# HGRN2 attention with both directions in one interleaved tile, 1024-wide DeltaNet steps, and modulation sums that end before HGRN2

## The chip, the cores and the metric

The kernel runs on one core of one Trainium2 chip. The metric is the device time of one execution in microseconds (us), the median of several runs. TensorE does the matrix products (PE in the rows, PEld for its weight loads), VectorE (DVE) and ScalarE (ACT) the elementwise work, GpSimd (POOL) a few memsets and part of the transfers, SyncE (SP) issues most of the transfers.

## The reference

One layer of a hybrid block over 256 latent tokens of width 2048, with 256 context tokens ahead of them. A modulation, computed from a conditioning vector by a product with `w_ada`, scales and shifts the tokens; one projection `w_in` feeds three token mixers: Hyena (a long convolution through a Fourier transform), HGRN2 (a gated linear recurrence, forwards and backwards) and a gated DeltaNet (forwards and backwards). Their outputs are projected, gated, merged and normalised; a squared-ReLU MLP of width 8192 follows. Cut to what the change touches:

```python
mod = silu(c) @ w_ada + b_ada                 # six parts; parts 2..5 are needed after the mixers
# HGRN2, per head and direction, by chunks:
att = einsum('tk,sk,tsk->ts', q, k, exp(cumsum(log f)_t - cumsum(log f)_s), s <= t)
o   = (q * exp(cumsum)) @ state + att @ v     # the two directions are summed
# DeltaNet, per chunk of 64: (I + strict_lower(kb k^T * decay)) is inverted by substitution
```

## The kernel before

All products with weights are made in three passes: `wsplit` (L141) loads a block of 128x1024 floats (512 KB) into a `wraw` buffer through SP's queue (L143), ScalarE rounds it (`whi`, L138), VectorE takes the remainder (`wlo`, L139), and TensorE multiplies high by high, high by low and low by high. There are four `wraw` buffers, four `whi` and three `wlo`. `wload` (L162) is called for every such block; before its own load it advances side jobs.

A side job is a Python generator that `beside` puts in with a rate, `go_on` gives a new rate, and `finish` runs to its end on the spot. At rate 0.55 each `wload` emits 0.55 steps of the job ahead of its weight load. Program order is therefore written out by hand. The framework then fixes the order on each engine by a timeline of its own: among the instructions that are ready it takes the one that is earliest in program order, and so lower work can fill an engine that would stand.

The stages, in program order:

- the first modulation, then `dn_early` (L642): DeltaNet's keys, queries, values and gates, with 24 calls of `wload`.
- `hyena(0)` and `hyena(1)` (L835, called at L913 and L915): six projections each (24 calls of `wload`), the Fourier products, and 12 steps of `fill` (L811), each one block of the output gates (L799 to L801). 72 calls in all.
- `hgrn_group(g)` (L921) for four groups of two heads. Each projects values (L932 to L935), both forget gates (`proj_cm_ctx`, L218 to L220) and queries: 16 calls of `wload`, and in the last group eight more from `fill`. Then come eight levels `lv`. At level `lv` the 256 tokens are cut into pairs of blocks of `1 << lv` tokens, scaled keys `Kt` and queries `Qt` are made (L1021 to L1024), multiplied on TensorE in 128x128 pieces (L1030), and copied under a mask into `att` (L1032); the running products are then extended (L1047 to L1050). Left and right halves of the pairs are separate instructions of 256 columns.
- `dn_inverse` (L742) runs beside the HGRN2 groups at rate 1.3. Its first steps, `dn_systems` (L699), build the matrices `M`; then 62 substitution steps (L756 multiply, L757 add) follow, split in two where they would be wider than 512 columns, with `tmp` in the tag `k2` (six buffers, 512 columns each).
- the gates and `dn_late` (L1160), the branches, `w_out`, and the MLP.

The modulation sums are the side job `ada`, `ada_parts(range(6))` (L500, put in at L780). It has 6 parts of 16 steps. A step loads 512 KB of `w_ada` through SP's queue into a `wraw` buffer (L503; the load of the next step is issued ahead of it), and VectorE multiplies and adds it into `acc` (L514 for the first step of a part, L516 for the 15 others). The part's end stores `acc` through POOL's queue (L518). `acc` lives in the tag `k4`, which has one buffer. `ada` runs at rate 1.0 through `dn_early`, 0.55 through Hyena (L912), 0.1 through HGRN2 (L1074), 0.3 afterwards (L1327), and is finished at L1403, ahead of its use in `ada_cols` (L1122).

Of the kernel before, what the change touches and what calls it, by code (L numbers as in the profile page):

```python
# [11 lines left out]
U8 = mybir.dt.uint8  # L12
# [4 lines left out]
P = 128  # L17
D = 2048
KT = D // P
T = 256  # L20
# [60 lines left out]
def tile_block(ctx: ExitStack, tc: tile.TileContext, A: dict, out: bass.AP):  # L81
# [325 lines left out]
    masks = cst.tile([P, 7, P], U8, name="masks")  # L407
    masks_f = page("masks_f", (7, P))
    dma(out=masks_f, in_=A["masks"])
    nc.vector.tensor_copy(out=masks, in_=masks_f)  # L410
# [331 lines left out]
    def dn_inverse():  # L742

        yield from dn_systems()
        M = dn["M"]
        bI = dn["inst"][:, 1, :]
        for s_ in range(1, 63):
            n = 63 - s_
            parts = 1 if n * s_ <= 512 else 2
            m = -(-n // parts)  # L750
            for a in range(s_ + 1, 64, m):
                b = min(a + m, 64)
                shp = [P, b - a, s_]
                tmp = slot([P, 512], "k2", "tmp")
                tv = tmp[:, 0:(b - a) * s_].rearrange("p (a b) -> p a b", a=b - a)
                tt_(out=tv, in0=bc(M[:, a:b, s_:s_ + 1], shp), in1=bc(M[:, s_:s_ + 1, 0:s_], shp), op=MUL)  # L756
                tt_(out=M[:, a:b, 0:s_], in0=M[:, a:b, 0:s_], in1=tv, op=ADD)  # L757
# [154 lines left out]
    go_on("ada", 0.55)  # L912
# [8 lines left out]
    def hgrn_group(g):  # L921
# [16 lines left out]
        fs, ks = [], []  # L938
        for d, base in enumerate((C_FF, C_FB)):
            pss = proj_cm_ctx(base + g * 256)  # L940
            f, k = page("fk", (2, 512), (2, 512))
            for h in range(2):
                hd = d * 8 + 2 * g + h
                act(out=f[:, h, :], in_=pss[h], func=AF.Sigmoid)
                act(out=k[:, h, :], in_=pss[h], func=AF.Sigmoid, scale=-1.0)
                act(out=f[:, h, :], in_=f[:, h, :], func=AF.Identity, scale=oml[:, hd:hd + 1], bias=lb[:, hd:hd + 1])
                act(out=k[:, h, :], in_=k[:, h, :], func=AF.Copy, scale=oml[:, hd:hd + 1])
            ts_(out=f, in0=f, scalar1=1e-30, scalar2=None, op0=MAX)
            fs.append(f)
            ks.append(k)  # L950
# [5 lines left out]
        for d in range(2):  # L956
            f, k = fs[d], ks[d]
            cp = slot([P, 2, T], "k2", "cp")
            kd, kt_ = k[:, :, T:2 * T], f[:, :, T:2 * T]
            for h in range(2):  # L960
                fc = f[:, h, T:2 * T]
# [23 lines left out]
        PF, SB = fs[0][:, :, 0:T], fs[1][:, :, 0:T]  # L985
        kf, kb_ = ks[0][:, :, 0:T], ks[1][:, :, 0:T]
        SF, PB = ks[0][:, :, T:2 * T], ks[1][:, :, T:2 * T]
        QF, QB = fs[0][:, :, T:2 * T], fs[1][:, :, T:2 * T]
        tt_(out=ksum, in0=kf, in1=kb_, op=ADD)
        ps = sc_ps()  # L990
        for h in range(2):
            for i in range(2):
                sl = slice(i * P, (i + 1) * P)
                mm(ps[:, (2 * h + i) * P:(2 * h + i + 1) * P], ksum[:, h, sl], q[:, h, sl], start=True, stop=True)
        copy(out=att.rearrange("p a b -> p (a b)"), in_=ps)

        def halves(t, b):
            v = t.rearrange("p h (n two b) -> p h n two b", two=2, b=b)
            return v[:, :, :, 0, :], v[:, :, :, 1, :]

        for lv in range(8):
# [3 lines left out]
            n = T // (2 * b)  # L1005
            Kt = slot([P, 2, T], "k2", "Kt")
            Qt = slot([P, 2, T], "k2", "Qt")
            PFl, PFr = halves(PF, b)
            SBl, SBr = halves(SB, b)
            SFl, SFr = halves(SF, b)  # L1010
            PBl, PBr = halves(PB, b)
            kfl, _ = halves(kf, b)
            _, kbr = halves(kb_, b)
            ql, qr = halves(q, b)
            Ktl, Ktr = halves(Kt, b)
            Qtl, Qtr = halves(Qt, b)
            if lv == 0:
                copy(out=Ktl, in_=kfl)
                copy(out=Ktr, in_=kbr)
            else:  # L1020
                tt_(out=Ktl, in0=kfl, in1=SFl, op=MUL)  # L1021
                tt_(out=Ktr, in0=kbr, in1=PBr, op=MUL)
            tt_(out=Qtl, in0=ql, in1=SBl, op=MUL)
            tt_(out=Qtr, in0=qr, in1=PFr, op=MUL)  # L1024
            ps = sc_ps()
            if lv < 7:
                for h in range(2):
                    for i in range(2):
                        sl = slice(i * P, (i + 1) * P)
                        mm(ps[:, (2 * h + i) * P:(2 * h + i + 1) * P], Kt[:, h, sl], Qt[:, h, sl],  # L1030
                           start=True, stop=True)
                nc.vector.copy_predicated(out=att, mask=bc(masks[:, lv:lv + 1, :], [P, 4, P]),  # L1032
                                          data=ps.rearrange("p (a b) -> p a b", a=4))
# [6 lines left out]
            shp = [P, 2, n, b]  # L1040
            if lv == 0:
                copy(out=SFl, in_=PFr)
                nc.gpsimd.memset(SFr, 1.0)
                copy(out=PBr, in_=SBl)
                nc.gpsimd.memset(PBl, 1.0)
            elif lv < 7:
                tt_(out=SFl, in0=SFl, in1=bc(PFr[:, :, :, b - 1:b], shp), op=MUL)  # L1047
                tt_(out=PBr, in0=PBr, in1=bc(SBl[:, :, :, 0:1], shp), op=MUL)
            tt_(out=PFr, in0=PFr, in1=bc(PFl[:, :, :, b - 1:b], shp), op=MUL)
            tt_(out=SBl, in0=SBl, in1=bc(SBr[:, :, :, 0:1], shp), op=MUL)  # L1050
        tt_(out=QF, in0=q, in1=PF, op=MUL)
        tt_(out=QB, in0=q, in1=SB, op=MUL)
# [21 lines left out]
    go_on("ada", 0.1)  # L1074
# [252 lines left out]
    go_on("ada", 0.3)  # L1327
# [215 lines left out]
```

## Time and profile before

| | us |
|---|---|
| three runs, lowest, median, highest | 2389.09, 2390.69, 2390.93 |
| the profiled execution, its own time | 2387.84 |
| its span, first to last instruction | 2385.8 |

| engine | busy us of the span | share | instructions |
|---|---|---|---|
| PE (matmul) | 2285.2 | 96% | 13377 |
| PEld (weight load) | 2003.1 | 84% | 13377 |
| DVE | 1624.5 | 68% | 2119 |
| ACT | 1053.3 | 44% | 1401 |
| POOL | 181.0 | 8% | 297 |

Busy time is the sum of the instructions' spans on an engine. Instructions of one engine overlap at their ends, so what one costs in a dense row of its like is the distance from one start to the next, which is shorter than its own duration. A granted clock (PEclk) of 1.00 is TensorE at 2.4 GHz, 0.5 is 1.2 GHz. One TensorE product of two plain fp32 operands shows as two matmuls in the trace.

### The profile page before, as it was taken

The page shows a single profiled execution, that of the slowest core. Times are in us where ns is not written, and L with a number is a line of the kernel's source. Part 1 is how long each engine was busy: PE and PEld are TensorE (multiplying, and loading weights), DVE is VectorE, ACT ScalarE, POOL GpSimd, SP SyncE. Part 2 cuts the span into 40 slices and gives each one's busy share as a digit, 9 for nine tenths or more (in the row PEclk, how much of TensorE's full clock was granted, in tenths as well). Part 3 has the DMA queues.
Part 4 walks back from the last instruction along what each step waited for, and adds up shares of the span by engine and source line. Part 5 has one row for each costly group of instructions (what it writes and reads, how often), then busy time and mean ns, then how long its engine had stood idle before and what let it go on. Part 6 is the DMA issues. An engine that isn't in the chain of part 4 may idle for free.

```text
span 2385.8 us, 34393 instructions
## 1 busy us (share of the span) xinstructions
PE 2285.2 (96%) x13377; PEld 2003.1 (84%) x13377; DVE 1624.5 (68%) x2119; ACT 1053.3 (44%) x1401; POOL 181.0 (8%) x297
## 2 busy tenths in 40 slices
PE   6999898999999999989999999997999999999998
PEld 4778688989889989777888888886988988988986
DVE  6776467867889898976656656658954555555557
ACT  6665444433433433534443444434444444444442
POOL 0000222000210000012021020000000000000000
PEclk9999999999999999989999999998999999999999
DMA  9958757777663333488786898677876566666664
GB/s 329 344 178 258 229 176 224 242 248 245 196 176 106 116 89 115 124 209 275 227 261 214 284 324 261 202 233 275 303 245 193 181 190 193 181 192 191 191 202 150
DMA packets 296079, 511.30 MB, mean 214 GB/s; under 512 B 17526, under 2 KB 155217, under 8 KB 293324
## 3 DMA queue, kind: packets, MB, share of 16 engines
q1 hardware_dynamic: 271488, 422.63, 56.0%
q0 software_dynamic: 21648, 82.01, 11.1%
q10 hardware_dynamic: 2780, 4.47, 0.5%
q8 instruction: 105, 1.72, 0.3%
q14 instruction: 58, 0.48, 0.1%
HBM read 474.59 MB, written 34.45 MB: 213 GB/s over the span
## 4 chain that ended last, share of the span: by engine, by line
PE 68%; DMA 8%; DVE 5%; ACT 1%; issue 1%; DVEq 0%; SPq 0%; POOL 0%; ACTq 0%
PE mm L220 8%; PE mm L219 8%; PE mm L218 8%; PE mm L475 8%; PE mm L476 8%; PE mm L474 8%; DMA aw<-in_w_ada_dram 3%; PE mm L800 3%; PE mm L801 3%; PE mm L799 3%; DMA wraw<-in_w_in_dram 2%; DVE wlo L139 2%; PE mm L932 1%; PE mm L935 1%; PE mm L934 1%
## 5 line engine op out<-in xcount | busy, mean ns | idle before, releaser
L138 ACT CAST whi<-wraw 128x1024 fp32r<-128x1024 f32 x584 | 613.3, 1052 | 955.0 <-PE mm L219 274.2
L139 DVE TENSOR_TENSOR wlo<-wraw,whi 128x1024 fp32r<-128x1024 f32 x584 | 712.1, 1222 | 452.4 <-PE mm L475 159.6
L220 PE MATMUL mm<-uh,wlo 128*128 128x256 f32 (+1 forms) x1024 | 340.6, 336 | 3.1 <-DVE wlo L139 3.1
L218 PE MATMUL mm<-uh,whi 128*128 128x256 f32 (+1 forms) x960 | 318.3, 332 | 13.8 <-DVE cy L490 13.2
L219 PE MATMUL mm<-ul,whi 128*128 128x256 f32 (+1 forms) x960 | 318.2, 332 | 0.0
L218 PE MATMUL mm<-u,whi 128*128 128x256 f32 x1024 | 290.6, 284 | 5.1 <-ACT u L138 3.8
L219 PE MATMUL mm<-u,whi 128*128 128x256 f32 x1024 | 290.4, 284 | 1.1 <-DVE u L139 1.1
L220 PE MATMUL mm<-u,wlo 128*128 128x256 f32 x1024 | 290.0, 284 | 0.7 <-DVE wlo L139 0.7
L220 PEld LDWEIGHTS mm<-uh,wlo 128*128 128x128 f32 x1024 | 198.3, 194 | 22.4 <-DVE wlo L139 3.8
L218 PEld LDWEIGHTS mm<-uh,whi 128*128 128x128 f32 x960 | 186.5, 194 | 31.1 <-issue 13.9
L218 PEld LDWEIGHTS mm<-u,whi 128*128 128x128 f32 x1024 | 197.4, 193 | 5.8 <-ACT u L138 4.2
L219 PEld LDWEIGHTS mm<-ul,whi 128*128 128x128 f32 x960 | 186.4, 194 | 15.4 <-issue 0.7
L219 PEld LDWEIGHTS mm<-u,whi 128*128 128x128 f32 x1024 | 197.3, 193 | 1.6 <-DVE u L139 1.4
L220 PEld LDWEIGHTS mm<-u,wlo 128*128 128x128 f32 x1024 | 197.0, 193 | 1.1 <-DVE wlo L139 1.1
L476 PE MATMUL mm<-whi,h 128*128 128x512 f32 x480 | 187.2, 390 | 0.0
L475 PE MATMUL mm<-wlo,h 128*128 128x512 f32 x480 | 186.8, 389 | 0.0
L474 PE MATMUL mm<-whi,h 128*128 128x512 f32 x480 | 186.5, 391 | 0.0
L516 DVE SCALAR_TENSOR_TENSOR acc<-aw,csil,acc 128x1024 f32<-128x1024 f32 x90 | 115.2, 1280 | 89.0 <-DMA aw<-in_w_ada_dram 88.7
L800 PE MATMUL mm<-wlo,uh 128*128 128x512 f32 x384 | 152.9, 398 | 4.3 <-DVE wlo L139 4.1
L799 PE MATMUL mm<-whi,uh 128*128 128x512 f32 x384 | 150.1, 400 | 3.3 <-ACT whi L138 1.7
L801 PE MATMUL mm<-whi,ul 128*128 128x512 f32 x384 | 151.2, 394 | 0.0
L474 PEld LDWEIGHTS mm<-whi,h 128*128 128x128 f32 x480 | 90.1, 188 | 19.2 <-issue 0.7
(517 smaller groups left out, 4113.9 us busy)
## 6 DMA issues: line engine op xcount, KB each, us to landing
wraw<-in_w_in_dram SPq DMA_DIRECT2D x264, 512.0 KB, 4.4
wraw<-in_w_ff_dram SPq DMA_DIRECT2D x256, 512.0 KB, 4.0
aw<-in_w_ada_dram SPq DMA_DIRECT2D x96, 512.0 KB, 4.4
raw<-in_w_ada_dram SPq DMA_DIRECT2D x32, 1024.0 KB, 5.6
wraw<-in_w_branch_dram SPq DMA_DIRECT2D x48, 512.0 KB, 5.4
wraw<-in_w_out_dram SPq DMA_DIRECT2D x32, 512.0 KB, 4.8
awr<-in_w_ada_dram SPq DMA_DIRECT2D x32, 512.0 KB, 9.4
g_d<-gate POOLq DMA_DIRECT2D x24, 256.0 KB, 4.6
```

Of the source, the lines that this page charges most:

```text
L138: copy(out=hi, in_=src)
L139: tt_(out=lo, in0=src, in1=hi.bitcast(F32), op=SUB)
L218: mm(ps, wh[:, k, cs], ah, start=first, stop=False, skip_group_check=True)
L219: mm(ps, wh[:, k, cs], al, start=False, stop=False, skip_group_check=True)
L220: mm(ps, wl[:, k, cs], ah, start=False, stop=last, skip_group_check=True)
L474: mm(pss[i], a, wh[:, k, :], start=(kt == 0), stop=False)
L475: mm(pss[i], a, wl[:, k, :], start=False, stop=False)
L476: mm(pss[i], b, wh[:, k, :], start=False, stop=(kt == nk - 1))
L516: stt(out=acc, in0=a, scalar=csil[:, 0, kt:kt + 1], in1=acc, op0=MUL, op1=ADD)
L799: mm(pg[i], a, wh[:, k, :], start=(kt == 0), stop=False)
L800: mm(pg[i], a, wl[:, k, :], start=False, stop=False)
L801: mm(pg[i], c, wh[:, k, :], start=False, stop=(kt == KT - 1))
```

## The change

It has three parts that lie close together in time.

1. HGRN2. The forget gates and keys of both directions go into two tiles `F` and `K` of [2 directions, 2 (latent, context), 2 heads, 256]. `pairs` builds one view that takes the left halves from one direction and the right halves from the other, so that each pair of instructions becomes one of 512 columns. Levels 0 to 5 need only the 64x64 blocks on the diagonal: `blocks` makes eight products with 64 stationary columns and 64 moving ones instead of four of 128 by 128, and the masked copy covers 256 columns instead of 512. Level 6 takes the off-diagonal blocks and writes the full `att` by four copies on ScalarE.
2. DeltaNet. Each substitution step is one multiply and one add, up to 1024 columns wide; `tmp` is taken once and lies in the tag `k4`, with `acc` of the modulation sums.
3. The modulation sums go at 0.61 per `wload` through Hyena instead of 0.55, and `finish("ada")` stands ahead of the first HGRN2 group. The later rates and the `finish` in `modulation2` go away.

```diff
-    masks = cst.tile([P, 7, P], U8, name="masks")
+    masks = cst.tile([P, 6, 64], U8, name="masks")
...
+        tmp = slot([P, 1024], "k4", "tmp")
         for s_ in range(1, 63):
             n = 63 - s_
-            parts = 1 if n * s_ <= 512 else 2
-            m = -(-n // parts)
-            for a in range(s_ + 1, 64, m):
-                b = min(a + m, 64)
-                shp = [P, b - a, s_]
-                tmp = slot([P, 512], "k2", "tmp")
...
+            shp = [P, n, s_]
+            tv = tmp[:, 0:n * s_].rearrange("p (a b) -> p a b", a=n)
+            tt_(out=tv, in0=bc(M[:, s_ + 1:, s_:s_ + 1], shp), in1=bc(M[:, s_:s_ + 1, 0:s_], shp), op=MUL)
+            tt_(out=M[:, s_ + 1:, 0:s_], in0=M[:, s_ + 1:, 0:s_], in1=tv, op=ADD)
             yield
...
-    go_on("ada", 0.55)
+    go_on("ada", 0.61)
     hyena(0)
     fill(0)
     hyena(1)
...
+        F = slot([P, 2, 2, 2, T], "k8", "F")
+        K = slot([P, 2, 2, 2, T], "k8", "K")
...
+        def pairs(t, left, right, b, step=1):
+            v = t[:, 0, 0, 0, 0:1]
+            return bass.AP(tensor=v.tensor, offset=v.offset + left,
+                           ap=[list(v.ap[0]), [2 * b, T // b], [right - left, 2], [step, b]])
+        def blocks(ps, lhs, rhs, other):
+            for h in range(2):
+                for i in range(2):
+                    for f in range(2):
+                        c = i * P + f * 64
+                        r = i * P + (1 - f if other else f) * 64
+                        mm(ps[f * 64:(f + 1) * 64, (2 * h + i) * 64:(2 * h + i + 1) * 64],
+                           lhs[:, h, c:c + 64], rhs[:, h, r:r + 64], start=True, stop=True)
...
-                tt_(out=Ktl, in0=kfl, in1=SFl, op=MUL)
-                tt_(out=Ktr, in0=kbr, in1=PBr, op=MUL)
-            tt_(out=Qtl, in0=ql, in1=SBl, op=MUL)
-            tt_(out=Qtr, in0=qr, in1=PFr, op=MUL)
+                tt_(out=Ktv, in0=pairs(K, KF, KB + b, b), in1=pairs(K, SF, PB + b, b), op=MUL)
+            tt_(out=Qtv, in0=qv, in1=pairs(F, SB, PF + b, b), op=MUL)
             ps = sc_ps()
-            if lv < 7:
...
+            if lv < 6:
+                blocks(ps, Kt, Qt, False)
+                nc.vector.copy_predicated(out=att64, mask=bc(masks[:, lv:lv + 1, :], [P, 4, 64]),
+                                          data=ps[:, 0:T].rearrange("p (a b) -> p a b", a=4))
+            elif lv == 6:
+                blocks(ps, Kt, Qt, True)
+                for f in range(2):
+                    fs, os = slice(f * 64, (f + 1) * 64), slice((1 - f) * 64, (2 - f) * 64)
+                    copy(out=att[fs, :, fs], in_=att64[fs])
+                    copy(out=att[fs, :, os], in_=ps[fs, 0:T].rearrange("p (a b) -> p a b", a=4))
...
     beside("inverse", dn_inverse(), 1.3)
-    go_on("ada", 0.1)
+    finish("ada")
     for g in range(4):
         hgrn_group(g)
...
-    go_on("ada", 0.3)
...
-        finish("ada")
```

## Rows read from the trace of the kernel before

**Rows 1.** Windows: window, its us, busy us (instructions), granted clock, DMA share, GB/s.

```profile
core 0: us, PE busy (x) PEld busy (x) DVE busy (x) ACT busy (x) POOL busy (x), PEclk, DMA share, GB/s
613.00:671.00 58.00, 58.00 (x371) 52.96 (x370) 39.55 (x41) 23.08 (x26) 15.36 (x17) 1.00 0.68 200
740.00:960.00 220.00, 220.00 (x1415) 200.38 (x1414) 199.36 (x371) 86.15 (x129) 1.33 (x4) 1.00 0.34 99
1000.00:1020.00 20.00, 14.72 (x60) 10.99 (x59) 19.32 (x18) 17.84 (x20) 3.08 (x7) 0.91 0.79 185
1040.00:1060.00 20.00, 13.40 (x55) 10.84 (x54) 15.26 (x33) 6.30 (x8) 0.00 (x0) 0.74 0.56 160
1100.00:1120.00 20.00, 17.92 (x88) 12.96 (x87) 13.25 (x18) 5.88 (x8) 4.72 (x10) 1.00 1.03 346
1420.00:1440.00 20.00, 19.61 (x87) 15.92 (x86) 11.30 (x12) 7.37 (x7) 1.61 (x3) 1.00 0.95 351
```

**Rows 2.** Chain that ended last: start us, us, what.

```profile
531.55 1.30 DVE acc L516
...
553.83 1.30 DVE acc L516
...
1027.32 17.71 DMA wraw<-in_w_in_dram
...
1345.83 8.07 DMA aw<-in_w_ada_dram
```

**Rows 3.** Line L516 up to 613 us: durations min/median/max ns, first and last start.

```profile
L516 DVE SCALAR_TENSOR_TENSOR acc<-aw,csil,acc x60: 1150/1283/1287, 153.1 to 611.6; 128x1024 f32<-128x1024 f32 x60
```

**Rows 4.** Page, DMA issues: count, KB each, median us to landing.

```profile
aw<-in_w_ada_dram SPq DMA_DIRECT2D x96, 512.0 KB, 4.4
```

**Rows 5.** Timeline of SP's queue around 613 us: start us, us, line, count.

```profile
609.37 77.11 SPq L143 DMA_DIRECT2D wraw<-in_w_in_dram  x15
687.25 6.06 SPq L503 DMA_DIRECT2D aw<-in_w_ada_dram  x2
```

**Rows 6.** Groups on PE from 613 to 671 us: count, busy us, mean ns.

```profile
L932 PE MATMUL mm<-whi,uh 128*128 128x256 f32 x64 | 18.1, 283 | 0.0
...
L218 PE MATMUL mm<-uh,whi 128*128 128x512 f32 x15 | 5.8, 390 | 0.0
```

**Rows 7.** Timeline of PE at two places: start us, us, line, shape, count.

```profile
733.23 0.28 PE L935 MATMUL mm<-whi,ul 128*128 128x256 f32 x1
733.35 1.06 PE L1030 MATMUL ps<-Qt,Kt 128*128 128x128 f32 x8
734.16 0.36 PE L932 MATMUL mm<-whi,uh 128*128 128x256 f32 x1
734.36 0.28 PE L934 MATMUL mm<-wlo,uh 128*128 128x256 f32 x1
...
1121.57 0.39 PE L800 MATMUL mm<-wlo,uh 128*128 128x512 f32 x1
1121.80 0.39 PE L801 MATMUL mm<-whi,ul 128*128 128x512 f32 x1
1122.12 1.14 PE L1205 MATMUL ps<-XT,VT 64*64 64x64 f32 x16
1123.10 1.09 PE L1200 MATMUL ps<-XN,CT 64*64 64x64 f32 x16
1124.12 0.50 PE L799 MATMUL mm<-whi,uh 128*128 128x512 f32 x1
```

**Rows 8.** Timeline of DVE at two places: start us, us, line, shape.

```profile
626.21 0.68 DVE L876 TENSOR_TENSOR cm<-ps,spl 128x512 f32<-128x512 f32 x1
626.81 0.68 DVE L877 TENSOR_TENSOR cm<-ps,spl 128x512 f32<-128x512 f32 x1
...
1054.83 0.41 DVE L1024 TENSOR_TENSOR Qt<-ivq,fk 128x256 f32<-128x256 f32 x1
1055.16 0.41 DVE L1047 TENSOR_TENSOR fk<-fk 128x256 f32<-128x256 f32 x1
1055.50 0.72 DVE L1032 COPY_PREDICATED hgA<-masks,ps 128x512 f32<-128x512 uint8 x1
```

**Rows 9.** Line L756, the substitution's multiply: durations min/median/max ns, first and last start.

```profile
L756 DVE TENSOR_TENSOR tmp<-M x106: 217/588/686, 687.1 to 996.7; 128x440 f32<-128x440 f32 x6, 128x486 f32<-128x486 f32 x4, 128x480 f32<-128x480 f32 x4, 128x468 f32<-128x468 f32 x4
```

More of the change, by code (lines that the diff above doesn't have):

```diff
@@ L404, in tile_block @@
         step()
-    masks = cst.tile([P, 7, P], U8, name="masks")
+    masks = cst.tile([P, 6, 64], U8, name="masks")
     masks_f = page("masks_f", (7, P))
     dma(out=masks_f, in_=A["masks"])
-    nc.vector.tensor_copy(out=masks, in_=masks_f)
+    for f in range(2):
+        fs = slice(f * 64, (f + 1) * 64)
+        nc.vector.tensor_copy(out=masks[fs], in_=masks_f[fs, 0:6, fs])
     colB = rows_to_cols([
@@ L937, in hgrn_group @@
             copy(out=iv[:, 2 * i:2 * i + 2, :].rearrange("p a b -> p (a b)"), in_=pss[i])
-        fs, ks = [], []
+        F = slot([P, 2, 2, 2, T], "k8", "F")
+        K = slot([P, 2, 2, 2, T], "k8", "K")
         for d, base in enumerate((C_FF, C_FB)):
             pss = proj_cm_ctx(base + g * 256)
-            f, k = page("fk", (2, 512), (2, 512))
             for h in range(2):
                 hd = d * 8 + 2 * g + h
[L944 to L950, printed above, removed]
+                f, k = F[:, 1 - d, :, h, :], K[:, d, :, h, :]
+                pv = pss[h].rearrange("p (s t) -> p s t", s=2)
+                act(out=f, in_=pv, func=AF.Sigmoid)
+                act(out=k, in_=pv, func=AF.Sigmoid, scale=-1.0)
+                act(out=f, in_=f, func=AF.Identity, scale=oml[:, hd:hd + 1], bias=lb[:, hd:hd + 1])
+                act(out=k, in_=k, func=AF.Copy, scale=oml[:, hd:hd + 1])
+            ts_(out=F[:, 1 - d], in0=F[:, 1 - d], scalar1=1e-30, scalar2=None, op0=MAX)
         pq = proj_cm(w_in, C_HQ + g * 256, uxh, uxl)
@@ L982, in hgrn_group @@
             copy(out=S0[:, :, d, :], in_=ps[:, 0:2 * P].rearrange("p (h v) -> p h v", h=2))
[L985 to L989, printed above, removed]
-        ps = sc_ps()
[L991 to L999, printed above, removed]
+        SB, PF, KF, KB, SF, PB = 0, 4 * T, 0, 4 * T, 2 * T, 6 * T
+        def pairs(t, left, right, b, step=1):
[10 more added lines that the diff above has]
+                           lhs[:, h, c:c + 64], rhs[:, h, r:r + 64], start=True, stop=True)
+        tt_(out=ksum, in0=K[:, 0, 0], in1=K[:, 1, 0], op=ADD)
+        ps = sc_ps()
+        blocks(ps, ksum, q, False)
+        att64 = ksum.rearrange("p h t -> p (h t)")[:, 0:T].rearrange("p (a b) -> p a b", a=4)
+        copy(out=att64, in_=ps[:, 0:T].rearrange("p (a b) -> p a b", a=4))
         for lv in range(8):
@@ L1004, in hgrn_group @@
             b = 1 << lv
-            n = T // (2 * b)
             Kt = slot([P, 2, T], "k2", "Kt")
             Qt = slot([P, 2, T], "k2", "Qt")
[L1008 to L1016, printed above, removed]
+            Ktv, Qtv, qv = (t.rearrange("p h (n two b) -> p (h n) two b", two=2, b=b) for t in (Kt, Qt, q))
             if lv == 0:
-                copy(out=Ktl, in_=kfl)
-                copy(out=Ktr, in_=kbr)
-            else:
-                tt_(out=Ktl, in0=kfl, in1=SFl, op=MUL)
-                tt_(out=Ktr, in0=kbr, in1=PBr, op=MUL)
-            tt_(out=Qtl, in0=ql, in1=SBl, op=MUL)
-            tt_(out=Qtr, in0=qr, in1=PFr, op=MUL)
+                copy(out=Ktv, in_=pairs(K, KF, KB + b, b))
+            else:
+                tt_(out=Ktv, in0=pairs(K, KF, KB + b, b), in1=pairs(K, SF, PB + b, b), op=MUL)
+            tt_(out=Qtv, in0=qv, in1=pairs(F, SB, PF + b, b), op=MUL)
             ps = sc_ps()
-            if lv < 7:
[L1027 to L1033, printed above, removed]
+            if lv < 6:
[4 more added lines that the diff above has]
+                blocks(ps, Kt, Qt, True)
+                for f in range(2):
+                    fs, os = slice(f * 64, (f + 1) * 64), slice((1 - f) * 64, (2 - f) * 64)
+                    copy(out=att[fs, :, fs], in_=att64[fs])
+                    copy(out=att[fs, :, os], in_=ps[fs, 0:T].rearrange("p (a b) -> p a b", a=4))
             else:
@@ L1039, in hgrn_group @@
                 copy(out=attx.rearrange("p a c b -> p (a c b)"), in_=ps)
-            shp = [P, 2, n, b]
             if lv == 0:
[L1042 to L1045, printed above, removed]
+                copy(out=pairs(K, SF, PB + b, b), in_=pairs(F, PF + b, SB, b))
+                nc.gpsimd.memset(pairs(K, SF + b, PB, b), 1.0)
             elif lv < 7:
[L1047 to L1052, printed above, removed]
+                t = pairs(K, SF, PB + b, b)
+                tt_(out=t, in0=t, in1=pairs(F, PF + 2 * b - 1, SB, b, 0), op=MUL)
+            t = pairs(F, SB, PF + b, b)
+            tt_(out=t, in0=t, in1=pairs(F, SB + b, PF + b - 1, b, 0), op=MUL)
+        qf = q.rearrange("p h t -> p (h t)").unsqueeze(1)
+        tt_(out=F[:, :, 1].rearrange("p d h t -> p d (h t)"), in0=bc(qf, [P, 2, 2 * T]),
+            in1=F[:, :, 0].rearrange("p d h t -> p d (h t)"), op=MUL)
+        QB, QF = F[:, 0, 1], F[:, 1, 1]
         ps = sc_ps()
```

8 lines of the change are left out of this document (2 added, 6 removed).

## The prediction, made blind

> **What bounds the kernel now.** I read the busy time by stage first, then the chain that ended last, then the queue that feeds the weights, then single instructions. In the heart of HGRN2 TensorE is busy for all of 220 us (740 to 960) at full clock [rows 1], and its matmuls of 512 columns start 0.23 us apart, those of 256 columns 0.12 us apart, with nothing between [rows 7]. VectorE is busy for 199 of the same 220 us, and the DMA engines for a third. So TensorE sets the pace there, and VectorE is close behind. TensorE stands idle at a few places after it: 5.3 us in 1000 to 1020, 6.6 us in 1040 to 1060 (where the granted clock means 0.74) and 2.1 us in 1100 to 1120 [rows 1]. The chain names transfers there: a weight load that took 17.7 us, and later a load of the modulation sums of 8.1 us [rows 2]. Whatever makes VectorE faster can pay only at such places; whatever takes weights away from TensorE costs at once.
>
> **The change, part by part.**
>
> **The modulation sums (part 3)** are the large term. There are 96 loads of 512 KB [rows 4]. By 613 us the trace shows 60 steps of the second to sixteenth kind [rows 3], which are four whole parts with their four first steps: 64 of 96. The program gives the same: 24 calls at 1.0 and 72 at 0.55 are 63.6, and one step is pulled ahead. At 0.61 they are 24 + 43.9, so 67 steps end with Hyena, one more load is under way, and `finish` emits the other 29 steps and 28 loads in one block ahead of every instruction of the first HGRN2 group. In the trace of before, SP's queue sends 15 weight loads between 609 and 687 us before the next two loads of the sums, and the first HGRN2 weights are among these 15 [rows 5]. All weights of the groups now queue behind the 28 loads, in the same four buffers. On VectorE 29 steps of 1.28 us, 37 us, stand ahead of the group's remainders and of `dn_systems`; on POOL's queue two stores of `acc` do. The second part in the block can't start adding until the store of the first has landed, since `acc` has one buffer; the four buffers are then full and the queue waits.
>
> How long the block lasts: 28 loads of 0.524 MB at the best rate in these rows, 351 GB/s at 1420 to 1440 us [rows 1], take 42 us. I add 5 us for the store between the parts (a median load lands in 4.4 us [rows 4]). So the group's first weights leave 47 us later, and TensorE needs another 7 us for landing (4.4 us), rounding and remainder (VectorE's remainder is about as long as a step of the sums); before, the first load left well ahead of its use. What covers these 54 us: in 613 to 671 TensorE was busy for all 58 us, and the group's own matmuls take 3 x 64 x 0.12 = 23 us and 3 x 15 x 0.23 = 10 us of them [rows 6, 7]; L934 and L935 are there as often as L932, L219 and L220 as often as L218. The other 25 us are the tail of Hyena and its gate blocks, whose weights are loaded. TensorE then stands for 54 - 25 = 29 us. Bounds: zero, if group loads get in between; 144 us, if each load waits for the step before it as in 531 to 554 us, where four steps took 22.3 us, 5.6 us each [rows 2]. I take 29, nearer the lower end, since that slow pace belongs to a queue that shared its buffers with weights. After such a stand the clock falls, as in 1040 to 1060 us: the missing quarter of 20 us is 5 us; I add 4 (0 to 5).
>
> Inside Hyena four more steps go in. Each held a buffer for one turn of a queue in which TensorE is nearly fed: +2 us (from 0, if hidden, to 4 x 5.6 = 22, if each costs a whole turn of those in 531 to 554 us).
>
> **The 64x64 blocks (part 1, TensorE).** Before, a level's four products are eight matmuls that start 0.81 us before the next line's, which gives up 0.08 us more: 0.89 us [rows 7]. After, sixteen matmuls of 64x64. The nearest rows have them: sixteen of L1205 and sixteen of L1200 go in 2.00 us; entering costs 0.32 - 0.23 = 0.09 us more than a normal start, leaving is taken to cost the same, so one block is 0.09 + 16 x 0.06 + 0.09 = 1.14 us. That is +0.25 us for each of 8 blocks (one ahead of the levels, levels 0 to 6) in 4 groups: +8 us on an engine that has no slack there. Upper bound: a matmul costs the same with half the columns, 16 x 0.11 + 0.18 = 1.94 us, +34 us in all. Lower bound: the two column halves run side by side, 0.66 us, -7 us in all. I take the measured pace.
>
> The Trainium skill (TensorEngine Tiling (Array Packing), sections Key Properties and Theoretical Speedup) says both things: that a change of tiling mode drains TensorE, and that disjoint halves may run in parallel, up to twice as fast. The trace agrees with the first (0.09 us on entering); the second no row here shows, because the eight products of those rows all lie on one tile. By the second the term would be the lower bound.
>
> **VectorE (parts 1 and 2).** Two instructions of 256 columns take 2 x 0.33 us, start to start, one of 512 takes 0.60 [rows 8], so a merge saves 0.07 us. There are 29 merges a group (2 at level 0, 4 at each of levels 1 to 6, 3 at level 7), 2.0 us. Masked copies shrink: 0.72 us each by their own duration; six at half width save some 2 us, and the seventh goes away. That makes 4.7 us a group, 19 us. The substitution goes from 106 to 62 pairs [rows 9]: 88 instructions x 0.07 = 6 us. The strided views cost nothing more in the rows at hand (0.41 us for both kinds of 1055 us); a view that jumps between two far places at each element is not in the trace, and if it ran at half speed it would eat all of this. Ten steps of the sums that ran between 690 and 1100 us are gone as well: 12 us. So VectorE loses 37 us of work in this stage. Under a TensorE that is busy throughout, none of it is worth anything between 740 and 960 us; there the cover is TensorE's own work, 220 of 220 us.
>
> It counts where TensorE stood. In 1000 to 1060 us the idle 5.3 + 6.6 us and the clock's share (0.09 and 0.26 of 20 us) are 18.9 us. These hang on the end of the inverse, whose last steps and transfers fall into the weights of the last group. An inverse that ends earlier meets projections that ask for half as many weights per us: I take 12 of the 18.9 (0 to 18.9). Later places where the sums' loads stood in the chain (1100 to 1120, 1346): -4 (0 to -6). ScalarE's changes (two copies fewer at level 0, four more at level 6) lie on an engine busy for 39% there: nothing, and if that cover went, sixteen copies at an estimated 0.4 us, VectorE's duration for as many columns, 6 us.
>
> `tmp` in one buffer makes no wait, since multiply and add follow on one engine; but its first use waits for the last store of `acc`. The block of sums ends at about 613 + 47 us, and the substitution began at 687 us: nothing, and what is late next, if it slips, is only the inverse.
>
> **Sum:** 29 + 4 + 2 + 8 - 12 - 4 = +27 us on 2387.84 us, 2414.8. The three runs have their median 2.85 us above the profiled execution: 2417.
>
> **The rivals.** (A) VectorE really bounds HGRN2, and the change pays. For it: 199 of 220 us, and remainders sit between TensorE and its weights. Then the block costs only what VectorE itself stands in it, 47 + 4 - 37 = 14 us, the blocks on TensorE cost nothing, and 37 us of work come off: 14 + 2 - 37 - 4 = -25, 2366 us with the 2.85. It decides if matmuls in 740 to 960 us start later than their own pace allows; the starts 0.12 and 0.23 us apart speak against it.
>
> On this the Trainium skill (Perfetto Trace Analysis, section Identifying the Most-Contended Engine) is sharper than busy time: it calls matmul busy share a poor measure and asks for the weight loads' share, and has the engine of highest occupancy improved first. By it TensorE (200 of 220 us of weight loads) and VectorE (199) stand level, and rival A has its reason; the trace does not decide it beyond the starts.
>
> (B) The block is mostly hidden: the scheduler lets group weights in between, or Hyena's tail is long enough. The gap falls to 6 us without the clock's loss: 6 + 2 + 8 - 16 = 0, 2391 us. For it: the DMA engines are only 68% busy in 613 to 671 us [rows 1]. Against it: program order puts all 28 loads first, and a load of the sums is ready whenever a buffer is free.
>
> (C) The block runs at 5.6 us a step, as in 531 to 554 us. 28 x 5.6 + 5 + 7 - 25 = 144 us of standing: 2387.84 + 144 + 14 - 16 + 2.85, 2533 us.
>
> **How the numbers follow.** No change is within 0.2%, about 4.8 us, which is what a measurement of this kernel can tell: 2385.9 to 2395.5. My forecast has a chance of 0.58, with 2397 to 2442 as its own range (the gap from 12 to 50 us, the blocks and the recovery as bounded); A has 0.24, spread from 2350 to 2385; B 0.12; C 0.06. Faster is A, 0.24; same is B, 0.12; slower is the forecast and C, 0.64. The range leaves out C, half of A and 0.02 of the forecast, 0.20: 2366 to 2444.
>
> **What would show it.** Right: SP's queue sends 28 loads of the sums in a row ahead of the first weights of HGRN2; TensorE stands for some 29 us at about 640 to 675 us with a granted clock below 1.00; sixteen-matmul blocks take 1.1 us; VectorE's share in the groups falls below 0.85 while TensorE stays at 1.00; the stand around 1000 to 1060 us shrinks. The forecast is wrong if group weights come in between the 28 loads, or if the time from the first to the last group shrinks by more than the recovery, which would mean that VectorE set the pace.

## The result, and the profile after

The kernel after takes 2432.94 us (median of 4 runs, 2428.36 to 2436.24), the kernel before 2390.81 in the same comparison: ratio 1.017, 95% interval 1.0145 to 1.0195. The profiled execution has a span of 2432.2 us against 2385.8: 46.4 us more.

Its windows (the columns are those of [rows 1]). The first and the fourth are stretches of [rows 1]; the last is a wider one, since everything from 704 us on lies some 72 us later than before:

```profile
613.00:671.00 58.00, 27.14 (x128) 22.64 (x127) 48.94 (x49) 11.89 (x14) 10.53 (x11) 0.75 0.72 218
671.00:703.00 32.00, 0.00 (x0) 0.00 (x0) 25.55 (x19) 0.00 (x0) 0.00 (x0) 0.50 0.63 212
703.00:740.00 37.00, 35.38 (x235) 33.42 (x236) 30.93 (x42) 10.52 (x11) 2.51 (x5) 0.90 0.63 183
740.00:960.00 220.00, 216.85 (x1485) 191.74 (x1483) 192.35 (x230) 88.49 (x132) 5.26 (x8) 0.99 0.36 100
960.00:1220.00 260.00, 258.80 (x1694) 221.60 (x1693) 160.04 (x191) 132.61 (x181) 30.71 (x45) 1.00 0.63 180
```

The wider window before:

```profile
960.00:1220.00 260.00, 245.71 (x1317) 205.40 (x1316) 186.40 (x272) 116.15 (x158) 40.76 (x64) 0.97 0.74 218
```

Between 613 and 703 us TensorE works for 27 us of 90, and in the last 32 us not at all, at a granted clock of 0.50 (1.2 GHz); before, it was busy for all of 613 to 671. The stands behind the groups are nearly gone: in 960 to 1220 us TensorE stands for 1.2 us at a granted clock of 1.00, against 14.3 us at 0.97 before. So the time is lost in one place and partly won back later. SP's queue around the loss (start us, us to the last issue, line, count), to be set beside [rows 5]:

```profile
605.33 2.26 SPq L143 DMA_DIRECT2D wraw<-in_w_in_dram  x2
609.60 86.52 SPq L505 DMA_DIRECT2D aw<-in_w_ada_dram  x28
697.11 18.06 SPq L143 DMA_DIRECT2D wraw<-in_w_in_dram  x8
```

The 28 loads go out in a row ahead of HGRN2's first weights, as forecast, but in 86.5 us instead of 47. HGRN2's first product, the first line of its values, is a milestone for all that follows (durations min/median/max, first and last start), before and after:

```profile
L932 PE MATMUL mm<-whi,uh x256: 277/283/365, 632.2 to 928.3; 128*128 128x256 f32 x128
```

```profile
L930 PE MATMUL mm<-whi,uh x256: 277/283/580, 704.2 to 1004.6; 128*128 128x256 f32 x128
```

It comes 72.0 us later. From there to the end of the span it is 2385.8 - 632.2 = 1753.6 us before and 2432.2 - 704.2 = 1728.0 after, so 25.6 us are won back: 72.0 - 25.6 = 46.4.

What stretched the loads, in the chain that ended last (start us, us, what):

```profile
660.07 14.99 DMA aw<-in_w_ada_dram
...
676.35 1.27 DVE M L718
...
680.84 1.20 DVE acc L518
682.04 1.12 DVE M L722
...
691.83 1.30 DVE acc L518
...
697.11 5.93 DMA wraw<-in_w_in_dram
```

One load of the sums takes 15 us; then work of `dn_systems` on M (L718, L722, L725) stands between a step at 680.84 and the next at 691.83; the loads wait for the buffers that those steps hold. At its own pace a step takes 1.3 us, as at 691.83. VectorE is busy for most of the block (columns of [rows 1]):

```profile
609.60:696.12 86.52, 30.54 (x140) 25.34 (x138) 72.52 (x68) 12.94 (x15) 10.53 (x11) 0.68 0.68 212
```

Of its 72.5 us some 31 are steps of the sums, some 21 the systems' work on E and M (L712 to L725), and some 20 work of Hyena. The transfers of 645 to 685 us show what shared the DMA engines with the slow load (count, KB each, median us to landing):

```profile
aw<-in_w_ada_dram SPq DMA_DIRECT2D x10, 512.0 KB, 3.5
M<-dk POOLq DMA_DIRECT2D x2, 1024.0 KB, 12.8
acc_d<-acc POOLq DMA_DIRECT2D x1, 512.0 KB, 2.9
br<-bth POOLq DMA_DIRECT2D x2, 256.0 KB, 16.2
```

### The profile page after: what moved, and what is told of

It is laid out like the page before. It is cut to its first block, busy times and chain, and to the rows that moved or that the text cites. A ratio compares the mean times of both kernels' runs of the same rounds, so it can differ in the third digit from the quotient of the medians.

```text
span 2432.2 us, 34716 instructions
## 1 busy us (share of the span) xinstructions
PE 2280.0 (94%) x13633; PEld 1993.9 (82%) x13633; DVE 1609.8 (66%) x1908; ACT 1061.2 (44%) x1409; POOL 180.6 (7%) x293
## 4 chain that ended last, share of the span: by engine, by line
PE 75%; DMA 11%; DVE 8%; issue 5%; ACT 2%; POOL 0%; ACTq 0%; DVEq 0%; SPq 0%; POOLq 0%
PE mm L218 9%; PE mm L219 9%; PE mm L220 9%; PE mm L477 7%; PE mm L478 7%; PE mm L476 7%; DMA aw<-in_w_ada_dram 6%; PE mm L798 3%; PE mm L799 3%; PE mm L797 3%; DMA wraw<-in_w_in_dram 2%; DVE acc L518 2%; DVE wlo L139 2%; PE mm L932 1%; PE mm L930 1%
## 5 line engine op out<-in xcount | busy, mean ns | idle before, releaser
L930 PE MATMUL mm<-whi,uh 128*128 128x256 f32 x256 | 74.3, 291 | 45.5 <-ACT whi L138 45.5
```

## The experiments

The theory after this reading: the third part makes the whole loss, stretched by the systems' work and M's load; the first two parts win. Twelve kernels were run. "First product" is that of HGRN2's values in the profiled run, "the rest" the span from there to the end, which shows the two effects apart. Ratios are to the kernel before on the same chip; its median there was 2385.08 to 2390.81 us, so totals of different rows compare only to within a few us. The two last columns are of one profiled run each.

| run | median us | ratio, 95% interval | first product | the rest |
|---|---|---|---|---|
| before | 2390.81 | 1 | 632.2 | 1753.6 |
| the whole change | 2432.94 | 1.017 (1.0145 to 1.0195) | 704.2 | 1728.0 |
| p3_only | 2441.75 | 1.0223 (1.0194 to 1.0253) | 708.1 | 1731.1 |
| p1_only | 2378.96 | 0.9958 (0.9944 to 0.9971) | 632.9 | 1746.3 |
| p12_page | 2376.08 | 0.9935 (0.9914 to 0.9956) | 625.9 | 1739.5 |
| inv_later | 2433.72 | 1.0189 (1.0156 to 1.0222) | 685.7 | 1745.9 |
| m_held | 2409.27 | 1.0108 (1.0085 to 1.0131) | 676.0 | 1730.1 |
| blocks128 | 2450.59 | 1.028 (1.0257 to 1.0304) | 703.7 | 1744.8 |
| rate100 | 2386.92 | 1.0007 (0.9995 to 1.0019) | 655.3 | 1731.6 |
| rate080 | 2399.37 | 1.0064 (1.004 to 1.0088) | 663.2 | 1734.5 |
| p12_spread | 2382.16 | 0.9975 (0.9962 to 0.9988) | 631.4 | 1746.3 |
| p12_r80 | 2379.94 | 0.9958 (0.9938 to 0.9977) | 641.5 | 1737.9 |
| half_order | 2441.47 | 1.0221 (1.0199 to 1.0243) | 708.3 | 1733.7 |
| p12_b128 | 2380.62 | 0.9965 (0.9952 to 0.9979) | 631.3 | 1748.1 |

### The parts by themselves

p3_only, on the kernel before:

```diff
-    go_on("ada", 0.55)
+    go_on("ada", 0.61)
...
-    go_on("ada", 0.1)
+    finish("ada")
...
-    go_on("ada", 0.3)
...
-        finish("ada")
         ada_cols()
```

> The kernel before with the third part alone: rate 0.61 in Hyena and the rest of the modulation sums in one block ahead of the first HGRN2 group; HGRN2 and the substitution as before. Theory (the block makes the whole loss and more, and the other two parts win some 27 us of it back): the first product of HGRN2's values starts near 704 us, as with the whole change, against 632 before; later the steps that are gone give back some 4 to 10 us, so the kernel takes 2450 to 2460 us. Rival (the block costs only what I forecast, 29 us and some clock, and the new blocks or the interleaved views lose the rest): first product near 665 us, 2415 to 2425 us. Second rival (the block is hidden without the other parts): within 5 us of 2391.

Measured: the first product at 708.1 us, so the block alone makes the delay; both rivals fall. The total is 8 us below my range, because 22.5 us are won back behind it although neither of the other parts is there.

p1_only is the whole change with its third part undone and the substitution as before:

```diff
-        tmp = slot([P, 1024], "k4", "tmp")
...
+                tmp = slot([P, 512], "k2", "tmp")
...
-    go_on("ada", 0.61)
+    go_on("ada", 0.55)
...
-    finish("ada")
+    go_on("ada", 0.1)
...
+    go_on("ada", 0.3)
...
+        finish("ada")
         ada_cols()
```

p12_page undoes the third part alone and has another home for `tmp`:

```diff
-        tmp = slot([P, 1024], "k4", "tmp")
+        tmp = page("tmp", (2048,))
```

> The first part alone: the interleaved tiles and 64x64 blocks of HGRN2; substitution in steps of 512 columns and the modulation sums at their old rates. Theory: the blocks give 6 to 7 us and VectorE's relief (13 us of its work in the groups) most of the 19 us that TensorE stood or was slowed at 1000 to 1060 us, so 2370 to 2384 us. Rival (the blocks or the interleaved views lose themselves): above 2391, with later starts of the second to fourth group. Second rival (VectorE sets HGRN2's pace throughout): more than 25 us gained, below 2366.

> The first and second part without the third: tmp of 1024 columns lies in one of the seven large pages, so that the modulation sums keep their own buffer and their old rates. Theory: 6.5 us from the blocks and the stands of TensorE from 1000 us on (some 19 to 27 us as the whole change shows them gone) give 2357 to 2368 us, faster than both kernels. Rival (parts one and two lose time of their own): above 2391. Second rival (the page that tmp holds makes the groups wait): slower than the first part alone by more than 3 us.

Measured: the first part gains 0.42%, and neither rival of p1_only holds. p12_page has the lowest time of all, 0.65% under the kernel before, though less was won than I expected: it missed its range. Its interval overlaps that of p1_only, so what the second part adds isn't clear of the noise. (Its profiled execution took 2367.1 us, the lowest of its six runs; its first product was 6 us early.)

So either cure wins time after the first product: 22.5 us in p3_only, 14.1 with the first two parts, and 25.6 with all. They remove much the same stands (columns of [rows 1]), first p3_only, then p12_page:

```profile
960.00:1220.00 260.00, 255.74 (x1527) 222.34 (x1526) 196.95 (x327) 124.62 (x170) 30.25 (x48) 0.99 0.61 176
```

```profile
960.00:1220.00 260.00, 251.63 (x1454) 209.11 (x1454) 162.64 (x186) 123.53 (x170) 46.34 (x70) 0.99 0.80 235
```

TensorE stands there for 14.3 us before, 4.3 in p3_only and 8.4 in p12_page. p3_only has no later steps of the sums. Its substitution also began with a head start, 10 us later than before (697.6 against 687.1 us) while the groups began 76 us later. The last start of the substitution's multiply tells when an inverse ends, here in p3_only, p12_page and inv_later (below):

```profile
L756 DVE TENSOR_TENSOR tmp<-M x106: 223/584/683, 697.6 to 1054.3; 128x440 f32<-128x440 f32 x6, 128x486 f32<-128x486 f32 x4, 128x480 f32<-128x480 f32 x4, 128x468 f32<-128x468 f32 x4
```

```profile
L754 DVE TENSOR_TENSOR tmp<-M x62: 224/936/1193, 698.5 to 942.2; 128x62 f32<-128x62 f32 x2, 128x122 f32<-128x122 f32 x2, 128x180 f32<-128x180 f32 x2, 128x236 f32<-128x236 f32 x2
```

```profile
L754 DVE TENSOR_TENSOR tmp<-M x62: 224/932/1199, 861.4 to 1084.0; 128x62 f32<-128x62 f32 x2, 128x122 f32<-128x122 f32 x2, 128x180 f32<-128x180 f32 x2, 128x236 f32<-128x236 f32 x2
```

Little of p3_only's head start is left at the end: 1054.3 - 708.1 = 346 us behind its first product, against 996.7 - 632.2 = 365 before [rows 9]. In inv_later the inverse ends 398 us behind it, and TensorE stands for 8.2 us of 1080 to 1120. In p12_page it ends 316 us behind it, and what is left is mainly one weight load of 14 us at 1057. No load of the sums goes out within 20 us before it; in 1055 to 1075 us POOL's queue, with loads of DeltaNet, had 69.6% of the DMA engines:

```profile
1057.59 14.24 DMA wraw<-in_w_in_dram
```

```profile
q0 software_dynamic: 1018, 3.49, 69.6%
```

m_held (below) has an inverse that ends as late as that of p12_page, 988.4 - 676.0 = 312 us behind the first product, but no later steps of the sums; its rest is 9.4 us shorter (1730.1 against 1739.5). So some 9 us of p12_page's rest go with those steps, by one profiled run each.

### What stretches the block

inv_later, on the whole change:

```diff
-    beside("inverse", dn_inverse(), 1.3)
     finish("ada")
     for g in range(4):
+        if g == 1:
+            beside("inverse", dn_inverse(), 1.75)
```

> The whole change, with the inverse put in only at the second group (rate 1.75 instead of 1.3), so that none of the systems' work (E, M, the load of M) stands among the steps of the block. Theory (the block's 28 loads last 86 us instead of 47 because VectorE's queue holds the systems' work between the steps): the loads of the block go out at 1.3 to 1.6 us each, 40 to 47 us in all, TensorE's stand at 653 to 703 us shrinks to 15 to 30 us, and the first product of the values starts at 665 to 682 us instead of 704; the total is below 2433 by up to 35 us, less what a later end of the inverse costs. Rival (the block's length is set by the transfers or by the four buffers alone): first product still at 698 to 708 us, total 2433 or more.

m_held, on the whole change:

```diff
         M = slot([P, 64, 64], "m16", "M")
+        nc.vector.tensor_copy(out=M[:, 0, 0:1], in_=dn["iv"][:, 0, 0:1])
...
+        if g == 0:
+            dn["iv"] = iv
+            beside("inverse", dn_inverse(), 1.4)
...
-    beside("inverse", dn_inverse(), 1.3)
     finish("ada")
```

> The whole change, with the inverse put in after the first group's values (rate 1.4), and one column of M written first from those values, so that the 2 MB load of M can't start during the block. With the inverse one group later the block's loads took 67 us, first product at 685.5 us, with one step that waited 10 us for its data while the 2 MB of M and 1 MB of branch stores were in the DMA engines. Theory (the block's rest over my 47 us is the systems' work on VectorE, some 18 us, and M's load in the transfers, some 10 us): the 28 loads go out in 47 to 58 us, and the first product starts at 666 to 678 us. Rival (the wait comes from the branch stores, the store between the parts or the four buffers): 684 us or later. The total is below 2433 if the inverse still ends in time, as it begins some 20 us later than with the whole change.

SP's queue in inv_later, then in m_held:

```profile
608.31 69.56 SPq L505 DMA_DIRECT2D aw<-in_w_ada_dram  x28
```

```profile
609.20 59.13 SPq L505 DMA_DIRECT2D aw<-in_w_ada_dram  x28
```

Without the systems' work the loads take 69.6 us, 17.0 less (the four profiled runs with the whole block and that work have 86.5 to 89.6), which falls between what the theory and the rival gave: neither the 47 us nor the unchanged block came true. What is left of the stretch in inv_later is one load, in its chain and with the shares of the queues from 650 to 668 us (packets, MB, share of the DMA engines; q0 carries POOL's transfers, q1 SP's):

```profile
650.49 15.56 DMA aw<-in_w_ada_dram
```

```profile
q0 software_dynamic: 253, 2.43, 59.0%
q1 hardware_dynamic: 587, 2.15, 38.9%
...
M<-dk POOLq DMA_DIRECT2D x2, 1024.0 KB, 15.1
```

M's load was still there: it went out at 650.5 us, released by a product of Hyena (L905), although the program puts it behind the first group. With it held back the loads take 59.1 us, 10.4 less again, and the first product is at 676.0, as the theory said; the burst itself is 1 us outside its range. What is left of it over 47 us is no longer a matter of transfers alone, as VectorE in m_held shows:

```profile
609.20:668.33 59.13, 29.70 (x139) 24.98 (x137) 48.88 (x54) 8.13 (x12) 3.79 (x7) 0.76 0.81 276
```

Of its 48.9 busy us some 31 are steps of the sums, and some 17 work of Hyena that stands between them. The total falls from 1.017 to 1.0108 of the kernel before. The total of inv_later missed, as it was no lower: its first product was 18.5 us earlier, but the inverse ended late, and its rest is 17.9 us longer.

### Fewer steps in the block

On the whole change, and the same with 0.8 for rate080:

```diff
-    go_on("ada", 0.61)
+    go_on("ada", 1.0)
```

> The whole change with the rate of the modulation sums in Hyena at 1.0 instead of 0.61: 24 + 72 steps, all 96 before HGRN2, so that no block is left. Theory (the block is the loss, and in Hyena a load hides as long as the transfers, busy for 0.63 to 0.78 of the time, have room): the stand at 640 to 700 us is gone, the first product of the values comes at 632 to 660 us, and with some 22 us won behind it because no steps are left there, 2355 to 2385 us. Rival (a step of the sums costs TensorE the same 1.5 to 2 us wherever it stands among weights that are nearly late): first product at 675 us or later, 2405 to 2435 us.

> The whole change with the rate 0.8 in Hyena: 81 steps with Hyena, 15 in the block instead of 29. Theory: the block shrinks by 14 steps of some 2.5 us, the first product comes at 655 to 680 us, 2385 to 2415 us in all, between the whole change and the rate of 1.0. Rival (a step costs the same wherever it stands): within 8 us of 2433.

```profile
615.97 39.59 SPq L505 DMA_DIRECT2D aw<-in_w_ada_dram  x14
```

Half the loads (14, this row is rate080) take 39.6 us, and the first product is at 663.2. With none left (rate100) it is at 655.3, 23.1 us later than before: 32 more steps than before cost Hyena 0.7 us each, which is neither free nor the 72 us of the block. The whole then stands level with the kernel before, 1.0007, a little over what the theory gave.

### The blocks on TensorE

blocks128 puts four products of 128x128, the masks of 128 columns and `att` back in levels 0 to 6 of the whole change; p12_b128 is the same edit on p12_page:

```diff
-            if lv < 6:
-                blocks(ps, Kt, Qt, False)
-                nc.vector.copy_predicated(out=att64, mask=bc(masks[:, lv:lv + 1, :], [P, 4, 64]),
-                                          data=ps[:, 0:T].rearrange("p (a b) -> p a b", a=4))
...
+            if lv < 7:
+                blocks(ps, Kt, Qt)
+                nc.vector.copy_predicated(out=att, mask=bc(masks[:, lv:lv + 1, :], [P, 4, P]),
+                                          data=ps.rearrange("p (a b) -> p a b", a=4))
```

> The whole change with the products of levels 0 to 6 back at 128x128, four to a level, and masked copies of 512 columns into att; the interleaved tiles stay. Theory (64x64 halves run side by side, 0.70 us a block against 0.89): TensorE loses 8 x 4 x 0.2 = 6.5 us, and VectorE, busy for 19 to 20 of every 20 us from 740 to 920, takes up to 4.7 us a group more: 2440 to 2452 us. Rival (my prediction: the blocks cost 1.14 us against 0.89): 2422 to 2428 us.

> The first and second part without the third, tmp in a page (2376.1 us with 64x64 blocks), and the products of levels 0 to 6 back at 128x128 with masked copies of 512 columns. By the starts of the matmuls a block of 128x128 costs 0.89 us and one of 64x64 0.81, 32 of them 3 us. Theory (TensorE sets the pace, and the wider copies on VectorE are hidden): 2377 to 2383 us. Rival (VectorE's wider copies, some 4 us a group, count too, as the 17.7 us of the same edit on the whole change suggest): 2388 to 2398 us.

half_order, on the whole change:

```diff
-            for h in range(2):
-                for i in range(2):
-                    for f in range(2):
+            for f in range(2):
+                for h in range(2):
+                    for i in range(2):
```

> The whole change, with the sixteen products of a block in another order: the eight of one 64-column half first, then the eight of the other, so that neighbours in the queue lie on the same half. Theory (the 0.031 us from start to start comes from neighbours on different halves that run side by side): spacing within a half near 0.06 us, a block 1.0 to 1.2 us instead of 0.70, 32 blocks and 10 to 14 us more of TensorE's time, 2436 to 2448 us. Rival (a matmul of 64 columns is simply that short): the same spacing of 0.031 us, 2430 to 2436 us.

The timeline of PE (start us, us, line, shape, count) in the kernel after, then in half_order:

```profile
823.50 0.39 PE L220 MATMUL mm<-uh,wlo 128*128 128x512 f32 x1
823.82 0.69 PE L999 MATMUL ps<-Qt,Kt 128*64 128x64 f32 x16
824.44 0.50 PE L218 MATMUL mm<-uh,whi 128*128 128x512 f32 x1
824.77 0.39 PE L219 MATMUL mm<-ul,whi 128*128 128x512 f32 x1
```

```profile
828.31 0.39 PE L220 MATMUL mm<-uh,wlo 128*128 128x512 f32 x1
828.63 0.97 PE L999 MATMUL ps<-Qt,Kt 128*64 128x64 f32 x16
829.52 0.50 PE L218 MATMUL mm<-uh,whi 128*128 128x512 f32 x1
829.86 0.39 PE L219 MATMUL mm<-ul,whi 128*128 128x512 f32 x1
```

From the first row of a fence to the last, less two normal starts of 0.23, a block costs 824.77 - 823.50 - 0.46 = 0.81 us in the kernel after and 829.86 - 828.31 - 0.46 = 1.09 us in half_order. Before, the same count gave 734.36 - 733.23 - 0.24 = 0.89 [rows 7]. So work on the two column halves does overlap, but only where neighbours in the queue lie on different halves; whether products overlap products or only weight loads do, these rows don't separate. That bears out the rule of the Trainium skill (TensorEngine Tiling (Array Packing), Key Properties), that different tiles can work in parallel. Thirty-two blocks save 32 x 0.08 = 2.6 us instead of costing 8. The order alone would cost 32 x 0.28 = 9.0 us; half_order's rest is 5.7 us longer than that of the whole change; its block and its total lie in the ranges of the theory. The other 4.1 us of its loss by the profiled runs came ahead of its first product, where no block is: the loads of the sums began 3.0 us later there (612.62 against 609.60), in a part of the program that is the same in both, and took 1.2 us longer. So most of it is scatter between executions; HGRN2's first weights went out 7.0 us earlier in p12_page than in p1_only (603.06 against 610.03), with the same program up to there.

The total of blocks128 is at the top of its range, but not for the reason I gave. Its chain holds one weight load of 23 us, which the whole change doesn't have, at 1139 us:

```profile
1138.88 23.34 DMA wraw<-in_w_in_dram
```

```profile
q0 software_dynamic: 1210, 4.43, 54.8%
```

The second row is POOL's queue in 1135 to 1165 us. As in p12_page it carries loads of DeltaNet; why they meet the weights at this place in blocks128 was not settled. On p12_page the same edit costs 4.5 us by the medians and 8.6 us in the rest. The total is within the theory's range. With 2.6 us for the blocks, 2 to 6 are left for VectorE's wider copies, so they are largely hidden there.

### The search for a faster version

p12_spread and p12_r80 are p12_page with other rates for Hyena and HGRN2:

```diff
-    go_on("ada", 0.1)
+    go_on("ada", 0.45)
```

```diff
-    go_on("ada", 0.55)
+    go_on("ada", 0.8)
...
-    go_on("ada", 0.1)
+    go_on("ada", 0.2)
```

> The first and second part, tmp in a page, and the modulation sums spread: 0.55 in Hyena as before, 0.45 through HGRN2 (32 steps in 72 weight calls), so that none is left behind it. Theory (in HGRN2 the transfers are busy for a third only, and the first two parts gave VectorE some 25 us back; the stands at 1060 and later come from the sums' loads): the steps fit, and the kernel takes 2350 to 2372 us, the fastest of all. Rival (VectorE, busy for 115 of 120 us at 740 to 860 us in the run with both parts, becomes the bound with 26 more steps of 1.28 us): 2380 to 2410 us.

> The first and second part, tmp in a page, the modulation sums at 0.8 in Hyena and 0.2 through HGRN2 (81 + 14 steps). Theory: Hyena's 18 more steps cost some 9 to 12 us (the rate of 1.0 cost 23 us up to the first product of the values for 32 more), the stands behind HGRN2 give some 10 us back: 2368 to 2385 us, no better than the run with both parts alone. Rival (the later stands are worth 20 us beyond what both parts gave): below 2365.

p12_spread missed its range. The windows of it (columns of [rows 1]):

```profile
680.00:700.00 20.00, 16.14 (x60) 12.81 (x59) 19.82 (x16) 8.90 (x12) 0.49 (x1) 0.83 0.56 148
...
740.00:960.00 220.00, 218.33 (x1613) 194.30 (x1612) 210.03 (x252) 83.59 (x126) 2.71 (x3) 1.00 0.45 132
960.00:1220.00 260.00, 251.51 (x1451) 208.19 (x1450) 172.23 (x208) 128.14 (x174) 47.77 (x73) 1.00 0.75 214
```

The first of them in p12_page:

```profile
680.00:700.00 20.00, 19.64 (x88) 16.10 (x87) 19.87 (x17) 2.10 (x2) 2.01 (x4) 1.00 0.69 185
```

From 740 us on TensorE is fed in the groups even with VectorE busy for 210 of 220 us, so the rival's bound isn't there. The steps push the inverse's end from 942 to 990 us, but TensorE stands no longer behind the groups than in p12_page, 8.5 us of 960 to 1220 against 8.4. It stands at the start of HGRN2: 3.9 us of 680 to 700, at a granted clock of 0.83, against 0.4. There VectorE works on M from 676 to 693 us, between remainders of weights. That the stands behind the groups come from the sums' loads, as the theory had it, is not borne out. p12_r80 is where the theory put it. p12_page stays the lowest, at 2376.08 us, but its interval overlaps that of p12_r80.

## Why the prediction was right or wrong

**Sign and time.** Slower was right, and 2432.94 lies in the range and in the forecast's own range; the size was +42.1 us by the medians (+46.4 by the profiled executions) against +27. (2414.8 and 2.85 make 2417.7, where I wrote 2417.) That the sum came this near is partly luck: the gap was some 40 us longer than forecast, and the blocks and the recovery together some 21 us better.

**The gap (+29).** The place, the order of the loads, the cover (TensorE was busy for 27 us of the stretch, I had 25) and the 7 us from the first weight load to the first product (697.11 to 704.2) were right. Wrong was "28 loads ... take 42 us ... I add 5 us": 86.5 us. TensorE stood for 63 us of 613 to 703, outside the 12 to 50 us that I gave the gap. I took the block for a matter of transfers, and the 37 us of steps on VectorE for hidden under them, since the steps stand first in program order. But VectorE was busy for 72.5 of the 86.5 us, and work that I had put at nothing stood between the steps: the systems' work (17.0 us by inv_later) and some 20 us of Hyena's. And M's 2 MB, which POOL's queue sent in the middle of the block, took the DMA engines (10.4 us by m_held). The other 12 us over 47 were not taken apart; but VectorE's work in m_held's block, with Hyena's in it, is 48.9 us by itself, more than my whole 47. With 86.5 in place of 47 my own working gives 29 + 39.5 = 68.5, near the measured 72.0. I had looked at what queues behind the block, not at what could get into it.

**Rival C** stays false: undisturbed steps went at 1.3 us and the loads of the block at 86.5 / 28 = 3.1 us, not 5.6. **Rival B** too: nothing of the groups came in between.

**The clock (+4)** was right: a tenth of 703 to 740 us is 3.7 us. **Hyena (+2)** held: at 0.7 us a step (rate100) four steps are 3 us.

**The blocks (+8)** had the wrong sign: -2.6. "I take the measured pace" took it from rows whose products all lie on one tile; half_order, where neighbours lie on one half, has 1.09 us a block where I forecast 1.14. The lower bound was the right value in kind.

**The recovery (-12 and -4)** was 25.6 us with the clock's and the blocks' share in it; without them 25.6 + 3.7 - 2.6 = 26.7, just over my outer bound of 24.9. I gave 12 of the 16 to an earlier end of the inverse. That a late end costs agrees with inv_later (398 us behind the first product, a rest of 1745.9). But p3_only, with the old HGRN2 and substitution, wins 22.5 us, and its inverse ends at 346 us, hardly ahead of the 365 before. Among the runs without later steps of the sums the rest is 1728.0 us with an end at 225 us (928.8 - 704.2, the whole change), 1730.1 at 312 (m_held) and 1731.1 at 346 (p3_only). So with those steps gone the faster inverse was worth little, by these single runs. The undersized term is that of the later steps, to which I gave 4 us; the two cures overlap, and what each is worth in the whole change was not separated.

**Rival A** falls as a mechanism: TensorE is busy for 218.33 of 220 us in p12_spread with VectorE at 210. The time from the first to the last group didn't shrink either: 928.3 - 632.2 = 296.1 us before, 1004.6 - 704.2 = 300.4 after. VectorE's share in the groups fell to 192.35 of 220, 0.87, not below 0.85 as I had it. Where VectorE did set a pace is the block itself. The rival's sign would have come true without the third part, by the stands behind the groups.

## What to carry to other kernels

A block of work that is put "ahead" on one queue holds only that queue: list every engine and every DMA queue that it shares, and what is ready to get in between, before pricing it at its transfer rate. A side job that is nearly hidden at a low rate is cheapest left spread out; moving 29 steps in one block in front of a tight stage cost 72 us here, where taking them all at a higher rate cost 23. If two parts of a change need a resource of each other (here `tmp` took the buffer of `acc`), look for another home first: with a page for `tmp`, two parts won 0.65% and the third could be dropped. And a load that lands late needn't wait for its own queue's traffic: look at what the other queues move at that moment.

## What the runs showed of the hardware that I had not expected

Sixteen matmuls of 64 columns start within 0.46 us when neighbours lie on different column halves and within 0.74 us when they lie on the same one; nothing else was changed. And one 512 KB load of the sums, 4.6 us in the median, took 15 us beside 3 MB that POOL's queue moved (M's 2 MB and stores of Hyena's branch): in that stretch of inv_later POOL's transfers had 59% of the DMA engines and SP's 39%. The weight loads of 14 us in p12_page (69.6% for POOL's queue) and 23 us in blocks128 (54.8%) stand beside such transfers too.

The views that jump between two far places, which could have run at half speed, cost more only where they jump at each element. `Kt` (made by ScalarE at level 0) in one instruction of 512 columns takes as long as the plain ones of [rows 8]. Of `Qt` and of the update of `F`, 28 of 32 do; the other four, one in each group at level 0, where the blocks are of one token, take 0.85 to 0.88 and 1.11 to 1.14 us (durations min/median/max ns).

```profile
L1017 DVE TENSOR_TENSOR Kt<-K x28: 683/686/694, 796.6 to 1105.4; 128x512 f32<-128x512 f32 x28
```

```profile
L1018 DVE TENSOR_TENSOR Qt<-ivq,F x32: 683/686/877, 793.6 to 1106.0; 128x512 f32<-128x512 f32 x32
L1043 DVE TENSOR_TENSOR F<-F x32: 678/686/1136, 798.3 to 1106.7; 128x512 f32<-128x512 f32 x32
```
